# A hybrid attention trunk on one core: five of the query projections by seven products, and what is done around them

## The chip, the cores and the metric

One Trainium2 chip; the kernel uses one of its cores. The metric is the device time of one execution in microseconds, as a median over several runs. TensorE (PE in the profile) does the matrix products, with its weight loads counted apart as PEld; VectorE is DVE, ScalarE is ACT, GpSimd is POOL, SyncE is SP. Each engine works through its own list of instructions in order, and waits on semaphores for the others.

## The reference, cut to what matters

The input of 512 positions is prepended with 16 learned ones and goes through two layers. The first is gated linear attention, which the change does not touch. The second is differential attention in 8 heads, and this is what is computed there (`lam` and `scale` are numbers, `bias` depends on head and distance):

```python
proj = xn @ w_in                     # (528, 1024) @ (1024, 8192)
q, k, v, z = split(proj, 4)          # per head: two q and two k of 128 columns, v and z of 256
s = q_m @ k_m.T * scale + bias       # m = 0, 1; causal
p_m = softmax(s)
a = p_0 - lam * p_1
o = a @ v                            # per head, blocks of 128 queries
o = head_rms(o) * gnorm * (1 - lambda_init)
y = silu(z) * o
h = h + y @ w_out                    # then a final RMS norm, meta positions dropped
```

The 16 prepended positions need keys and values but no queries and no output, so q and z are made for 512 positions and k and v for 528.

## The kernel before, in words

**Numbers.** Every float32 operand of a product is split into a high and a low part (`split`, L276 to L280: ScalarE copies the rounded high part, VectorE subtracts it to get the low one), and a product is the sum high x high + high x low + low x high. `mm3` (L400) does this for small products.

**Two ways to project.** A projection takes 1024 inputs to 256 outputs for one head. `project` (L421) does it plainly: for each half of 128 outputs, 8 blocks of inputs by 3 passes, so 24 matmuls of 512 columns and 48 for a head. Class `Unit` does it as a two by two block product with seven half-sized products in place of eight (Winograd's form): `product` (L431) is one of the seven, 12 matmuls with half of the columns (256 for z, 264 for k and v). Three of the seven results are read out of PSUM by ScalarE (`partial`, L452) and joined to the others by VectorE (`add`, L477 and L479). The weights of a unit need, beside the split of two sums, four sums (`sums` and `outer`, L366) and the splits of three single blocks, `a11`, `a12` and `a22`; plain weights need two splits of 128x1024 only. The corresponding sums of the inputs are made once for all heads (`token_sums2`), and `Xr` is their part without the 16 meta positions. Units chain: a unit that has another behind it in the queue (`nxt`) runs that one's first product (`first`) before its own last ones. One that was begun so (`early`) and has no unit behind it is a lone one: it runs p6, p5, p7, p2, p4, p3. p6 and p7 go to the same PSUM bank `bx`, and p7 may not start before ScalarE has read what p6 left there (u2).

**Head by head.** In the loop over the eight heads the projections of the next head (z, v, k, q in that order; k, q, v, z for the last one) are put into a queue of generators, the `Weaver`. The attention of the present head is a list `steps` of A, B, C and E, each for the four blocks of 128 queries, the longest first. A (`scores`) makes the scores of both m by `mm3`, VectorE adds the bias and takes the minimum (L1692, as the q are negated), ScalarE takes the exponential with the row sums (L1694), VectorE makes the ratio `lam * sum0 / sum1` (L1697, L1698) and subtracts (L1699). B (`turn`) transposes the result on TensorE (L1707, L1708) and splits it. C (`values`) multiplies by v and takes the norm of the row (GpSimd's power -1/2 at L1730, ScalarE's scaling at L1731). E (`rows`) transposes one block (L1737), VectorE multiplies by the gate (L1740), and the result is split into `ys`. Between two steps `W.fill(us)` takes so many estimated microseconds of matmuls out of the queue, so TensorE's list is an order fixed by these shares. The output projection of a pair of heads, `q_diff_out2`, stands first in the queue of heads 2 to 6, so that a head begins with three of its banks and then A of the longest block.

**The other engines' lists.** TensorE's order is the program's. On VectorE, ScalarE, GpSimd and SyncE a scheduler places the instructions, with the priorities that `urgent`, `soon` and `at_once` give (at_once first, soon last). Weights come through SyncE's queue into two `raw` buffers; `Weights` makes the parts of at most two jobs ahead, as the buffers allow.

## Time and profile before

| what | value |
|---|---|
| median of 3 runs | 971.22 us (970.94 to 971.46) |
| the profiled execution: its time, its span | 970.65 us, 968.9 us |
| mean granted TensorE clock | 0.999 |
| PEld busy | 906.9 us (94%) |
| POOL busy, instructions | 44.9 us (5%), 68 |
| bytes moved by DMA | 104.94 MB, 108 GB/s |

The profiled execution's time is 1.75 us more than its span, and 0.57 us less than the median. The gated linear attention fills the first half, up to about 450 us; the scores of the eight heads begin at 500.1, 552.4, 605.0, 667.9, 730.9, 794.0, 857.0 and 911.8 us, so a head's pass is a stretch of about 63 us in the middle.

How to read it: "busy" of PE runs from a matmul's start to its modelled end, which overlaps the next one, so a PE at 100% need not be at its peak; the distance from one start to the next tells its rate. A group's row gives line, engine, operation, tiles and shapes, count, then busy time and mean duration, then the idle time of the engine just before and what ended it.

### The profile page before, as it was taken

What the parts mean: (1) busy time and instruction counts of PE and PEld (TensorE: products, weight loads), DVE (VectorE), ACT (ScalarE), POOL (GpSimd) and SP (SyncE); (2) the same over time, 40 slices, a digit from 0 to 9 for tenths busy, and PEclk for the clock granted to TensorE, in tenths of its full rate; (3) what the DMA queues carried; (4) which work ended last, traced back from release to release, by engine and by line L of the source; (5) the groups of instructions that cost most, each with busy time, mean ns of one, the idle gap of its engine ahead of it and who ended that gap; (6) DMA issues with size and microseconds to landing.
All of it is one profiled execution on the core that took longest, in us unless ns stands there. A gap on an engine that the chain in (4) does not pass through costs nothing.

```text
span 968.9 us, 18048 instructions
## 1 busy us (share of the span) xinstructions
PE 957.2 (99%) x6993; PEld 906.9 (94%) x6993; DVE 778.6 (80%) x1586; ACT 626.8 (65%) x1304; POOL 44.9 (5%) x68
## 2 busy tenths in 40 slices
PE   9999999999999999999999999999999999999997
PEld 8999999999999999998899998998999989989996
DVE  7989885886888787668997987968869769687785
ACT  7776755577647567656757776575675756755583
POOL 1000000000000000000001001000000000000001
PEclk9999999999999999999999999999999999999999
DMA  7322223635363236124355525243342341722212
GB/s 197 88 85 59 82 79 122 147 103 128 116 162 91 85 117 158 53 101 152 99 130 138 143 73 133 75 139 98 99 138 88 118 119 44 182 70 84 89 64 87
DMA packets 128522, 104.94 MB, mean 108 GB/s; under 512 B 51102, under 2 KB 112830, under 8 KB 128433
## 3 DMA queue, kind: packets, MB, share of 16 engines
q1 hardware_dynamic: 123104, 93.80, 35.1%
q10 hardware_dynamic: 5328, 9.95, 2.8%
q8 instruction: 56, 0.92, 0.4%
q14 instruction: 34, 0.27, 0.1%
HBM read 83.64 MB, written 11.80 MB: 99 GB/s over the span
## 4 chain that ended last, share of the span: by engine, by line
PE 88%; ACT 1%; DVE 1%; issue 1%; POOLq 0%; DVEq 0%
PE bx L431 19%; PE bv L431 12%; PE by L431 10%; PE bx L421 10%; PE ps L400 9%; PE bx L972 5%; PE bx L400 3%; PE bv L972 2%; PE by L972 2%; PE ps L1214 2%; PE by L400 2%; PE bv L400 2%; PE ps L1807 1%; PE bx L1807 1%; PE bv L421 1%; PE by L421 1%
## 5 line engine op out<-in xcount | busy, mean ns | idle before, releaser
L277 DVE TENSOR_TENSOR wl<-raw,wh 128x1024 fp32r<-128x1024 f32 x98 | 119.4, 1221 | 23.0 <-ACT wh L276 18.9
L276 ACT ACTIVATE wh<-raw 128x1024 fp32r<-128x1024 f32 x98 | 103.1, 1054 | 48.3 <-PE by L972 22.9
L431 PE MATMUL bv<-x,wh 128*128 128x264 f32 (+1 forms) x656 | 98.6, 287 | 0.0
L431 PE MATMUL bx<-x,wh 128*128 128x264 f32 (+1 forms) x640 | 95.6, 286 | 0.0
L431 PEld LDWEIGHTS bv<-x,wh 128*128 128x128 f32 x656 | 86.8, 189 | 0.6 <-DVE z L479 0.2
L431 PEld LDWEIGHTS bx<-x,wh 128*128 128x128 f32 x640 | 84.6, 188 | 0.7 <-ACT u L452 0.2
L452 ACT ACTIVATE u<-bx 128x264 f32<-128x264 f32 (+1 forms) x120 | 45.3, 379 | 35.5 <-PE bx L431 33.1
L1694 ACT ACTIVATE p<-p,st 128x528 f32<-128x528 f32 (+3 forms) x64 | 36.5, 570 | 41.7 <-DVE st L1692 41.4
L421 PE MATMUL bx<-x,wh 128*128 128x512 f32 (+1 forms) x256 | 62.4, 385 | 0.0
L277 DVE TENSOR_TENSOR wl<-sum,wh 128x1024 fp32r<-128x1024 f32 x41 | 50.1, 1221 | 10.6 <-ACT wh L276 10.5
L431 PE MATMUL bx<-x,wl 128*128 128x264 f32 (+1 forms) x320 | 54.1, 284 | 0.0
L431 PE MATMUL bv<-x,wl 128*128 128x264 f32 (+1 forms) x328 | 53.8, 284 | 0.1
L421 PEld LDWEIGHTS bx<-x,wh 128*128 128x128 f32 x256 | 44.4, 188 | 7.8
L276 ACT ACTIVATE wh<-sum 128x1024 fp32r<-128x1024 f32 x41 | 43.1, 1051 | 9.7 <-PE by L972 3.9
L431 PE MATMUL by<-x,a12h 128*128 128x264 f32 (+1 forms) x320 | 47.5, 286 | 0.1
L1730 POOL TENSOR_TENSOR st<-st,mhalf 128x1 f32<-128x1 f32 x32 | 25.5, 795 | 468.6 <-ACT on L1728 418.2
L431 PE MATMUL bx<-x,a11h 128*128 128x264 f32 (+1 forms) x320 | 46.6, 284 | 0.0
L431 PEld LDWEIGHTS bv<-x,wl 128*128 128x128 f32 x328 | 45.4, 188 | 0.3 <-issue 0.3
L431 PEld LDWEIGHTS bx<-x,wl 128*128 128x128 f32 x320 | 45.3, 188 | 0.3
L431 PEld LDWEIGHTS bx<-x,a11h 128*128 128x128 f32 x320 | 42.4, 188 | 0.6
L431 PEld LDWEIGHTS by<-x,a12h 128*128 128x128 f32 x320 | 42.1, 188 | 0.3 <-ACT t L1658 0.3
L276 ACT ACTIVATE a11h<-raw 128x512 fp32r<-128x512 f32 x41 | 25.7, 626 | 20.7 <-DMA raw<-in_diff_w_in_dram 7.9
(493 smaller groups left out, 2631.9 us busy)
## 6 DMA issues: line engine op xcount, KB each, us to landing
raw<-in_gla_w_in_dram SPq DMA_DIRECT2D x48, 512.0 KB, 4.5
raw<-in_diff_w_in_dram SPq DMA_DIRECT2D x42, 512.0 KB, 4.9
raw<-in_diff_w_in_dram SPq DMA_DIRECT2D x11, 1024.0 KB, 5.9
raw<-in_gla_w_out_dram SPq DMA_DIRECT2D x8, 1024.0 KB, 5.8
raw<-in_diff_w_out_dram SPq DMA_DIRECT2D x8, 1024.0 KB, 6.0
vd<-planes ACTq DMA_DIRECT2D x12, 268.0 KB, 5.8
vd<-keep ACTq DMA_DIRECT2D x12, 264.0 KB, 2.3
T<-bdr SPq DMA_DIRECT2D x8, 264.0 KB, 4.7
```

The source lines that it names most:

```text
L276: act.activation(hi, src, AF.Copy)
L277: dve.tensor_tensor(lo, src, hi.bitcast(F32), op=ALU.subtract)
L400: pe.matmul(ps, l, r, start=first and n == 0, stop=last and n == 2, **kw)
L421: pe.matmul(bank, a[:, k, :], b[k] if n0 is None else b[k][:, n0 + i * nn:n0 + (i + 1) * nn], start=n == 0 and ks[0] == 0, stop=n == len(t ...
L431: pe.matmul(bank[:, :x[q].shape[2]], w[p][:, k * P:(k + 1) * P], x[q][:, k, :], start=first and i == 0, stop=i == len(PASSES) - 1, skip_gr ...
L452: W.moved = act.activation(t, self.bx[:, :self.n], AF.Copy, scale=self.sc)
L972: pe.matmul(banks[i][:, :HT], h.t[p][:, k, mm * P:(mm + 1) * P], s.y[q][k][:, i * HT:(i + 1) * HT], start=n == 0, stop=n == len(PASSES) - 1)
L1214: pe.matmul(o, s.kd[:, i, kc], s.qs[:, i, t0:t0 + n], start=i == 0, stop=i == 1)
L1694: act.activation(p[:, :nk], p[:, :nk], AF.Exp, scale=-1.0, bias=st[:, m:m + 1], accum_out=st[:, 2 + m:3 + m])
L1730: pool.tensor_tensor(ms, ms, mhalf[:, :1], op=ALU.pow)
L1807: pe.matmul(ps[i], yp[hd][p][:, k, b * P:(b + 1) * P], wt[q][cs.start // 512][:, 2 * hd + k, cs.start % 512:(cs.stop - 1) % 512 + 1], star ...
```

## The change

Four things are edited.

1. `q_diff_q`: for heads 3 to 7 the query projection is a `Unit` on `Xr`, as z is, and no longer plain. Its result goes to two scratch tiles `t`, which are split into q with the lower priority of `soon`. Heads 0 to 2 stay plain. TensorE's list loses 240 matmuls of 512 columns and gets 420 of 256; all its other matmuls keep their number and shape, and k of these heads now has a unit behind it, so that q is the lone unit where k was (for head 7, v follows q, and z is the lone one as before). SyncE loads the same bytes of these weights as two transfers of 512 KB in place of one of 1 MB.
2. `scores`: m = 1 is done before m = 0, and the ratio is made by three GpSimd instructions on 128x1 (power -1 of the sum of m = 1, then two products) in place of VectorE's reciprocal and product. `minus` is a new constant.
3. `rows` takes two blocks together (heads 0 to 6): four transposes into one PSUM tile, one product with the gate on 128x512, one split. `steps` has 14 entries in place of 16.
4. The order: in a lone unit a step that is due within 1.6 us of the end of p5 is put just there, between p5 and p7 (`Gap`, `to_gap`, and `fill`). The fill at the start of a head is 4.0 in place of 3.0.

```diff
@@ Weaver.fill
             us -= c
             self.left -= c
             self.spent(c)
+            if isinstance(c, Gap) and us < 1.6:
+                return
+            if us <= 0 and 0 < getattr(self.queue[0], "to_gap", 0) < 1.6:
+                us = 0.01
...
@@ Unit.run
             def p5():
                 self.bv = pb_tile("bv")
-                yield from product(self.bv, ws.use(s21)[1], X["t1"])
+                alone = early and nxt is None
+                self.to_gap = 1.4 if alone else 0
+                for c in product(self.bv, ws.use(s21)[1], X["t1"]):
+                    self.to_gap -= c
+                    if alone and self.to_gap < 0.2:
+                        self.to_gap = 0
+                        c = Gap(c)
+                    yield c
...
     def q_diff_q(hd, s):
+        scale, qts = -float(P) ** -0.5, []
+
+        def tiles():
+            assert not hd or heads[hd - 1].scored
+            s.q = [T(ep, [P, 2, NR], F32R, f"q{j}", bufs=1) for j in range(2)]
+
+        if hd in (3, 4, 5, 6, 7):
+            def dst():
+                tiles()
+                qts.extend([tok_tile()[:, :NR], tok_tile()[:, :NR]])
+                return qts
+
+            @soon
+            def tail(i):
+                split(*[t[:, i, :] for t in s.q], qts[i])
+
+            return W.add(Unit(want_unit(d_w_in, 256 * hd), Xr, scale, dst, tail), 8.9)
         want_diff(256 * hd)
...
@@ scores
-            for m in range(2):
+            for m in (1, 0):
...
-            dve.reciprocal(st[:, 5:6], st[:, 3:4])
-            dve.scalar_tensor_tensor(st[:, 5:6], st[:, 5:6], lam, st[:, 2:3], op0=ALU.mult, op1=ALU.mult)
+                r.p[m] = p[:, :nk]
+
+            pool.tensor_tensor(st[:, 5:6], st[:, 3:4], minus, op=ALU.pow)
+            pool.tensor_tensor(st[:, 4:5], st[:, 2:3], lam, op=ALU.mult)
+            pool.tensor_tensor(st[:, 5:6], st[:, 5:6], st[:, 4:5], op=ALU.mult)
             dve.scalar_tensor_tensor(r.p[0], r.p[1], st[:, 5:6], r.p[0], op0=ALU.mult, op1=ALU.subtract)
...
-        def rows(r):
+        def rows(*rs):
+            w = P * len(rs)
             pt = ps_tile()
             for m in range(2):
-                pe.transpose(pt[:, m * P:(m + 1) * P], r.on[:, m * P:(m + 1) * P], ident)
-            y = T(ep, [P, 2, P], F32, "yt")
-            cs = slice(r.ta, r.ta + P)
-            W.mark = dve.tensor_tensor(y, pt[:, :256].rearrange("p (m c) -> p m c", m=2), s.z[:, :, cs], op=ALU.mult)
+                for j, r in enumerate(rs):
+                    pe.transpose(pt[:, m * w + j * P:m * w + (j + 1) * P], r.on[:, m * P:(m + 1) * P], ident)
+            y = T(ep, [P, 2, w], F32, "yt", bufs=1)
+            cs = slice(rs[0].ta, rs[0].ta + w)
+            W.mark = dve.tensor_tensor(y, pt[:, :2 * w].rearrange("p (m c) -> p m c", m=2), s.z[:, :, cs], op=ALU.mult)
             split(ys[hd][0][:, :, cs], ys[hd][1][:, :, cs], y)
...
-        return A, lambda b: turn(R[b]), lambda b: values(R[b]), lambda b: rows(R[b])
+        return A, lambda b: turn(R[b]), lambda b: values(R[b]), lambda b: rows(*([R[b]] if hd == D_HEADS - 1 else [R[b], R[b + 1]]))
...
-        steps = [(A, 0), (A, 1), (B, 0), (A, 2), (C, 0), (B, 1), (E, 0), (A, 3), (C, 1), (B, 2), (E, 1), (C, 2), (B, 3),
-                 (E, 2), (C, 3), (E, 3)]
+        steps = [(A, 0), (A, 1), (B, 0), (A, 2), (C, 0), (B, 1), (A, 3), (C, 1), (B, 2), (E, 1), (C, 2), (B, 3),
+                 (C, 3), (E, 3)]
...
-        W.fill(3.0)
+        W.fill(4.0)
```

Two places show how the lists move. The first is VectorE at the longest block of the scores of the fifth head's pass (`heads[4]`), before: `ISA p<-ps,T` is the sum with the bias and the minimum (its second row, on `st`, reads the minimum out), `st` holds the sums, `p` the scores.

```order
L1692 ISA p_12028,st_12015<-ps_12029,T_11624 128x264
L1692 ISA st_12015 128x1
L1692 ISA p_12028,st_12015<-ps_12034,T_11624,st_12015 128x264
L1692 ISA st_12015 128x1
L1697 RECIPROCAL st_12015<-st_12015 128x1
L1698 SCALAR_TENSOR_TENSOR st_12015<-st_12015,lam 128x1
L1699 SCALAR_TENSOR_TENSOR p_12016<-p_12028,st_12015,p_12016 128x528
L277 TENSOR_TENSOR wl_12052<-sum_11986,wh_12051 128x1024
```

The same place on VectorE in the changed kernel; L1734 there is L1699 of before, L592, L421 and L286 are splits of v, of its meta rows and of weights.

```order
L1726 ISA p_12142,st_12129<-ps_12148,T_11658,st_12129 128x264
L1726 ISA st_12129 128x1
L592 TENSOR_TENSOR v_2167_12119<-planes_11751,v_2166_12118 128x4x128
L421 SCALAR_TENSOR_TENSOR vm_12120<-lands_12080,short,vm_12120 32x256
L286 TENSOR_TENSOR a22l_12230<-raw_12082,a22h_12229 128x512
L1734 SCALAR_TENSOR_TENSOR p_12142<-p_12130,st_12129,p_12142 128x528
L286 TENSOR_TENSOR wl_12167<-sum_12100,wh_12166 128x1024
```

The two small instructions on `st` are gone, and three others stand between the last reading of the minimum and the subtraction; the subtraction now needs GpSimd's last product, and the split of the weights `wl` stands behind it.

The second place is TensorE in the lone unit of the same pass, before: `wh_11632,wl_11633` against x_1542 is p6, against x_1541 p5; bank `bx_11655` with x_1543 is p7, and L1737 are the transposes of E.

```order
L431 MATMUL bx_11655<-x_1542_8785,wh_11632 128x264 x5
L431 MATMUL bx_11655<-x_1542_8785,wl_11633 128x264 x4
L431 MATMUL bv_11757<-x_1541_8784,wh_11632 128x264 x8
L431 MATMUL bv_11757<-x_1541_8784,wl_11633 128x264 x4
L431 MATMUL bx_11655<-x_1543_8786,wh_11718 128x264 x3
L1737 MATMUL ps_11777<-ident,on_11685 128x128 x2
```

TensorE in the lone unit of the same pass in the changed kernel, which is q: again p6 and p5, then E of two blocks (L1774).

```order
L440 MATMUL bx_11891<-x_1542_8787,wh_11868 128x256 x8
L440 MATMUL bx_11891<-x_1542_8787,wl_11869 128x256 x4
L440 MATMUL bv_11986<-x_1541_8786,wh_11868 128x256 x8
L440 MATMUL bv_11986<-x_1541_8786,wl_11869 128x256 x4
L1774 MATMUL ps_11999<-ident,on_11944 128x128
L1774 MATMUL ps_11999<-ident,on_11854 128x128
```

Before, p7 followed p5 at once and the transposes came three matmuls into p7; now the four transposes stand whole between p5 and p7.

More of the change, by code (lines that the diff above doesn't have):

```diff
@@ L144, in settle @@
                 self.late.pop(0)[1]()
+class Gap(float):
+    pass
 class Part:
@@ L625, in trunk @@
     dve.memset(mhalf, -0.5)
+    minus = cp.tile([P, 1], F32, name="minus")
+    dve.memset(minus, -1.0)
     warm = ps_tile()
```

8 lines of the change are left out of this document (3 added, 5 removed).

## The prediction

> **What bounds the kernel now.** I read the page first, for the engines' shares.
>
> ```profile
> span 968.9 us, 18048 instructions
> PE 957.2 (99%) x6993; PEld 906.9 (94%) x6993; DVE 778.6 (80%) x1586; ACT 626.8 (65%) x1304; POOL 44.9 (5%) x68
> ```
>
> Then the busy time by stretch, cut at the first scores of four heads, since the change lies there.
>
> ```profile
> core 0: us, PE busy (x) PEld busy (x) DVE busy (x) ACT busy (x) POOL busy (x), PEclk, DMA share, GB/s
> 667.87:730.90 63.03, 63.03 (x436) 58.70 (x434) 49.96 (x109) 41.14 (x92) 2.97 (x4) 1.00 0.35 107
> 730.90:793.99 63.09, 63.09 (x435) 58.70 (x434) 48.76 (x108) 40.86 (x92) 3.15 (x4) 1.00 0.37 107
> 793.99:857.03 63.04, 63.04 (x435) 58.74 (x434) 48.92 (x107) 39.20 (x90) 2.61 (x4) 1.00 0.41 113
> ```
>
> TensorE has no idle time in a pass of 63.0 us, at full clock; VectorE rests for 13 to 14 us of it, ScalarE for 22 to 24. So a matmul taken from TensorE's list is time gained, as long as the others keep up. Since a busy PE can hide short waits, I took the rates from starts, in the chain of waits (first row: a plain q; the next two: a lone unit's p7 and the product behind it) and in TensorE's timeline (the rest).
>
> ```profile
> 787.14 2.79 PE bx L421 x12
> 529.24 1.63 PE bx L431 x12
> 530.88 1.47 PE by L431 x12
> ...
> 682.80 1.10 PE L431 MATMUL bv<-x,wh 128*128 128x256 f32 x8
> 683.74 0.64 PE L431 MATMUL bv<-x,wl 128*128 128x256 f32 x4
> 684.22 1.10 PE L431 MATMUL bx<-x,wh 128*128 128x256 f32 x8
> ```
>
> A matmul of 512 columns takes 2.79/12 = 0.2325 us. A product of 12 matmuls of 256 takes 684.22 - 682.80 = 1.42 us, 0.118 each.
>
> **TensorE's part.** For a changed head 48 x 0.2325 = 11.16 us go and 7 x 1.42 = 9.94 us come: 1.22 us less, 6.1 us for five. All other matmuls stay. This lies on the path, so the gain before losses is 6.1 us.
>
> The Trainium skill, "TensorE: Matmul & The Clock Gate", section "Back-to-back issue gap", speaks against this: it gives about 81 ns for a matmul of 128 columns and about 131 ns for one of 512 in a stream of weight loads and matmuls. By a straight line between these, an estimate, 256 columns would take 98 ns, and the sum would be 48 x 0.131 = 6.3 us gone and 84 x 0.098 = 8.2 us come. The rows above disagree for the long ones (232 ns), so the sum goes by the rows.
>
> **VectorE's part.** The groups by shape between 500 and 950 us, and one row of its waits there:
>
> ```profile
> L277 DVE TENSOR_TENSOR a11l<-raw,a11h 128x512 fp32r<-128x512 f32 x19 | 13.1, 689 | 9.3 <-ACT a11h L276 9.1
> L366 DVE TENSOR_TENSOR sum<-raw 128x512 f32<-128x512 f32 x19 | 13.0, 684 | 2.6 <-DMA raw<-in_diff_w_in_dram 2.6
> L280 DVE SCALAR_TENSOR_TENSOR q<-bx,q 128x512 fp32r<-128x512 f32 x14 | 9.6, 684 | 0.3 <-ACT q L279 0.3
> L277 DVE TENSOR_TENSOR hT<-yt,hT 128x256 fp32r<-128x256 f32 x22 | 9.2, 420 | 2.7 <-ACT hT L276 2.6
> L1698 DVE SCALAR_TENSOR_TENSOR st<-st,lam 128x1 f32<-128x1 f32 x32 | 6.9, 216 | 0.6
> L1697 DVE RECIPROCAL st<-st 128x1 f32<-128x1 f32 x32 | 5.1, 158 | 9.4 <-ACT p L1694 9.4
> L479 DVE TENSOR_TENSOR t<-by,u 128x256 f32<-128x256 f32 x7 | 2.9, 415 | 0.0
> ...
> DVE st L1697 <- ACT p L1694: 9.4, 11, 1.8
> ```
>
> A changed head adds three splits of single blocks (3 x 0.689), four sums of weights (4 x 0.684), four joinings (4 x 0.415) and two splits of q from scratch (as a block's, 2 x 0.689), and loses two of q from PSUM (2 x 0.684): +6.47 us. The weights' two big splits stay. Every head loses 4 x (0.216 + 0.158) = 1.50 us of ratios. Rows by twos: eight instructions of about 0.420 become four of 128x512, about 0.684: -0.62 us. So a pass with a changed q has 49.96 + 6.47 - 1.50 - 0.62 = 54.3 us of VectorE in 61.8 us, 88%.
>
> On top come waits. The subtraction of the scores (L1699) now needs ScalarE's exponential and then two GpSimd products in a row, and whatever VectorE has behind it stands too: weight splits, joinings that free PSUM banks for TensorE. From the timeline of the last short block, VectorE's reading of the minimum, the exponential, then GpSimd between two ScalarE instructions:
>
> ```profile
> 939.59 0.08 DVE L1692 DVE_READ_ACCUMULATOR2_ANT st<- 128x1 f32 x1
> 939.70 0.42 ACT L1694 ACTIVATE p<-p,st 128x144 f32<-128x144 f32 x1 [0.32 <-DVE st L1692]
> 940.02 0.18 ACT L1694 ACTIVATION_READ_ACCUMULATOR p<-p,st 128x1 f32 x1
> 940.63 0.19 ACT L1728 ACTIVATION_READ_ACCUMULATOR on<-ps 128x1 f32 x1
> 940.96 0.55 POOL L1730 TENSOR_TENSOR st<-st,mhalf 128x1 f32<-128x1 f32 x1 [7.17 <-issue]
> 941.54 0.47 ACT L1731 ACTIVATE on<-ps,st 128x256 f32<-128x256 f32 x1 [0.72 <-POOL st L1730]
> ...
> 570.63 2.27 POOL L1730 TENSOR_TENSOR st<-st,mhalf 128x1 f32<-128x1 f32 x1 [24.76 <-ACT on L1728]
> 570.67 1.22 DVE L277 TENSOR_TENSOR wl<-sum,wh 128x1024 fp32r<-128x1024 f32 x1
> ```
>
> From the minimum (939.67) to the sum (940.20) 0.53 us; to GpSimd 0.14; its instruction 0.55; back to another engine 0.03. A product on GpSimd isn't in the trace; the bounds are nothing and the 2.27 us above, and I take the 0.55 of a power. The power of m = 1 lies beside the exponential of m = 0. So the subtraction can start 0.53 + 0.14 + 2 x 0.55 + 0.03 = 1.8 us after the minimum of a short block, some 0.3 later for a long one. The new order puts none to three other instructions between, about 1.2 us on average by the durations above, so a wait of w = 0.6 to 0.9 us is left; I take w = 1.0, four in a pass. In place of it go the 9.4 us of L1697's waits in eight passes, 1.2 a pass. TensorE needs the result in B, at least one step and two fills later (over 5 us by its estimates), so it loses nothing directly.
>
> What does such a full VectorE cost TensorE? The fullest stretch of before is in the first layer, where units follow each other:
>
> ```profile
> 60.00:70.00 10.00, 10.00 (x84) 10.00 (x84) 10.00 (x18) 7.62 (x16) 0.00 (x0) 1.00 0.06 7
> 70.00:80.00 10.00, 9.85 (x81) 9.46 (x80) 9.79 (x18) 5.50 (x9) 0.00 (x0) 1.00 0.29 101
> 80.00:90.00 10.00, 9.85 (x83) 9.66 (x82) 9.60 (x18) 4.40 (x9) 0.00 (x0) 1.00 0.39 111
> ```
>
> VectorE at 29.4 of 30 us, TensorE idle 0.3: 1%. Over five new units of 10 us that is 0.5 us, my term for new losses. Its cover is the weights made ahead; without it a unit would wait for them.
>
> **ScalarE's part.**
>
> ```profile
> L276 ACT ACTIVATE a11h<-raw 128x512 fp32r<-128x512 f32 x19 | 11.8, 624 | 8.3 <-DMA raw<-in_diff_w_in_dram 7.9 <-PE bx L431 0.4
> L279 ACT ACTIVATE q<-bx 128x512 fp32r<-128x512 f32 x14 | 8.2, 586 | 0.4 <-PE bx L421 0.3
> L452 ACT ACTIVATE u<-bx 128x256 f32<-128x256 f32 x20 | 7.5, 377 | 13.0 <-PE bx L431 13.0
> ```
>
> Five copies (3 blocks, 2 of q) and three readings, less two of q: 5 x 0.624 + 3 x 0.377 - 2 x 0.586 = +3.1 us on 41 of 62: hidden by its 20 us of rest.
>
> **The rest.** The gap: the lone unit's p7 of the chain above took 1.63 us where its neighbour took 1.47, so at most 0.16 us a pass can go, 0.8 for five; four transposes there also cover for u2. I count nothing and keep 0.8 for the range. The fill of 4.0 takes as many pieces of the output projection (1.4 each, three pass 3.0 and 4.0) in heads 2 to 6, and moves order only elsewhere: nothing. Two transfers of 512 KB land no later than one of 1 MB; the queue before them is as long. At the end, A of the shortest block holds VectorE some 0.8 us longer (1.8 after the minimum where L1699 now starts 1.0 after it), beside TensorE's products: at most that, inside the range.
>
> **Sum.** 970.65 - 6.1 + 0.5 = 965.05 us for the profiled execution; from the median of 971.22 us, 5.6 less is 965.6 us.
>
> **Rivals.** *The seam of the heads.* The new q goes through joining, ScalarE and VectorE, with lower priority, before the next head's scores; TensorE has only three output banks in between. Before, in the timeline of all engines:
>
> ```profile
> 726.68 0.40 PE L400 MATMUL bx<-wh,y 128*128 128x512 f32 x1
> 728.17 0.58 ACT L279 ACTIVATE q<-bx 128x512 fp32r<-128x512 f32 x1
> 729.13 0.68 DVE L280 SCALAR_TENSOR_TENSOR q<-bx,q 128x512 fp32r<-128x512 f32 x1
> ```
>
> q's products end at 726.68, ScalarE comes 1.49 us later, q is ready at 729.81, 3.13 us after, and the scores start at 730.90: 1.09 us to spare. Joining adds about 0.2 + 0.415 and waits. For it: the queues that made these 1.49 us grow. Against: m = 1 now goes first, and its half of q comes a product (1.42 us) earlier, while m = 0 has its six scores of 264 columns more. If 0.8 us are lost at each of five seams, 4.0 of 5.6 us go: 969.6 us.
>
> *VectorE becomes the bound, slower.* A pass of VectorE is 54.3 + 4w + r, r being what it rests anyway; in the full stretch above 2%, 1.2 us. It passes 63.04 where w is over (63.04 - 54.3 - 1.2)/4 = 1.9 us. For it: GpSimd took 2.27 us beside VectorE's split. Against: VectorE stands still as it waits, which leaves GpSimd its 0.55. With no instruction between and a GpSimd product at 0.86, w = 2.5: 65.5 us a pass, 2.5 us more in each of five, 983.7 us.
>
> The Trainium skill, "SBUF — State Buffer", section "Who interferes with whom", has a VectorE instruction with two SBUF inputs and a GpSimd one that reads SBUF exclude each other, the first to start blocking the other. In the rows above GpSimd started first, and VectorE's split kept its 1.22 us: the trace bears out only half of it. By the whole rule three more GpSimd instructions a step would hold VectorE 4 x 3 x 0.55 = 6.6 us a pass, an estimate with the trace's duration, and bring this rival's point near without any w.
>
> *The short matmuls are dear.* More matmuls mean more weight loads, from the page's groups:
>
> ```profile
> L431 PEld LDWEIGHTS bv<-x,wh 128*128 128x128 f32 x656 | 86.8, 189 | 0.6 <-DVE z L479 0.2
> ```
>
> If 256 columns cost more than 11.16/84 = 0.133 us in q, the exchange loses. If a weight load sets the pace there, 84 x 0.189 = 15.9 us, 4.7 more a head, 23.6 in all: 994.8 us. The 0.118 of the same form in z, and the 0.136 of the slow p7, speak against it.
>
> By the Trainium skill's rule of the gap, above, the loss would be 1.9 us a head, and the time an estimated 981 us; the 232 ns of the long matmuls leave it little.
>
> *It doesn't do what it says*, TensorE's list unchanged: 971.2 us; the lists by themselves exclude it.
>
> **How the numbers follow.** About 0.2%, 1.9 us, can be told from no change. Forecast (better included) 0.76, the seam 0.12, VectorE 0.09, short matmuls 0.03. Of the seam's cases half are faster by over 0.2% (under 969.3 us) and half within: faster 0.82, same 0.06, slower 0.12. The low end is 971.22 - 6.1 - 0.8 and 0.3 for the spread of runs, 964.0; the high end is the seam's 969.7. Left out are VectorE, the short matmuls and some of either edge, under 2 in 10.
>
> **What would show it.** Right: a pass of about 61.9 us between first scores; L421 gone from heads 3 to 7; 256-column products at 1.42 us; VectorE at 54 us a pass; L1734 waiting for GpSimd about 1 us. Wrong: TensorE idle ahead of the first scores on q (the seam), or ahead of weights or banks on VectorE (the second), or L1734's waits near 2 us with passes over 63.

## The result, and the profile after

The changed kernel takes 974.16 us (median of 9 runs, 972.19 to 976.48), the kernel before on the same chip 970.94 us (970.35 to 971.46): a ratio of 1.0036, 95% interval 1.0025 to 1.0046. It is slower by a third of a per cent, where 965.6 us was forecast. The profiled execution took 974.99 us.

The shares of the engines, from the page of the changed kernel:

```profile
span 972.1 us, 18486 instructions
PE 953.7 (98%) x7173; PEld 911.9 (94%) x7173; DVE 795.6 (82%) x1550; ACT 637.1 (66%) x1320; POOL 82.9 (9%) x164
```

TensorE's busy time fell by 3.5 us, but its idle time (span less busy) rose from 968.9 - 957.2 = 11.7 us to 972.1 - 953.7 = 18.4. Busy time also hides short waits. The whole loss is the span's +3.2 us and the 6.1 us that TensorE's own work should have lost: 9.3 us. The stretches, cut at the first scores of the eight heads, show where it lies:

```profile
502.18:556.79 54.61, 53.01 (x388) 49.80 (x387) 42.95 (x90) 37.53 (x88) 8.13 (x16) 1.00 0.66 148
556.79:608.19 51.40, 51.40 (x367) 48.37 (x366) 40.72 (x87) 36.79 (x86) 8.84 (x16) 1.00 0.35 102
608.19:670.21 62.02, 62.02 (x471) 59.84 (x471) 51.62 (x103) 40.72 (x92) 8.52 (x16) 1.00 0.37 109
670.21:733.41 63.20, 62.40 (x471) 59.91 (x471) 55.53 (x112) 43.19 (x97) 7.61 (x16) 1.00 0.36 108
733.41:795.61 62.20, 62.12 (x471) 59.81 (x471) 53.57 (x106) 42.35 (x96) 7.86 (x16) 1.00 0.37 109
795.61:859.61 64.00, 62.45 (x472) 59.90 (x471) 52.71 (x107) 42.45 (x95) 7.79 (x16) 1.00 0.38 108
859.61:916.51 56.90, 56.28 (x387) 51.76 (x386) 49.24 (x97) 34.98 (x83) 7.18 (x16) 1.00 0.25 79
```

With 1.22 us less, the four passes of 62.9 to 63.1 us before should take 61.7 to 61.9. The third pass takes 62.02, 0.9 us less than its 62.90 before, so most of what the exchange is worth shows there; the next three lose about 1.4, 0.3 and 2.2 us again. The other losses lie at the ends. The first two passes take 106.0 us where 104.8 stood, although three pieces of a unit (9 matmuls of 264 columns, some 1.1 us) now come before the first scores: 2.3 us lost. The last two take 112.5 us where 111.87 - 1.2 was due: 1.8 us. The remaining 0.9 us lies before the first scores; profiled executions of kernels whose TensorE lists are the same up to there begin them between 499.7 and 500.7 us, so this is no sure loss.

What TensorE waited for between 500 and 960 us, in the view of waits (total, times, longest), before:

```profile
PE ps L400 <- DVE yt L1740: 0.2, 1, 0.2
```

and after:

```profile
PE bx L440 <- ACT u L461: 1.4, 2, 0.8
PE ps L409 <- DVE aT L286: 1.0, 1, 1.0
PE ps L409 <- ACT aT L285: 0.9, 2, 0.6
PE bv L440 <- DVE t L488: 0.7, 1, 0.7
PE ps L409 <- DVE am L419: 0.4, 1, 0.4
PE by L440 <- DVE t L486: 0.2, 1, 0.2
PE bx L409 <- DVE keep L1820: 0.2, 1, 0.2
```

They are several kinds of small waits, each for a reading, a split or a joining on ScalarE or VectorE, 4.8 us in all; the rest of the 9.3 us shows in no wait of this view. The largest kind, in the fourth pass, in the timeline of all engines (u is the reading of p6 that frees the bank for p7; the unit here is the first of the pass, that of z, which the change leaves as it was):

```profile
684.13 0.91 PE L409 MATMUL ps<-k,q 128*128 128x272 f32 x6
684.88 0.52 PE L440 MATMUL bx<-x,wl 128*128 128x256 f32 x3
685.30 0.68 DVE L375 TENSOR_TENSOR sum<-raw 128x512 f32<-128x512 f32 x1
685.90 0.43 DVE L1726 CUSTOM_DVE_ANT_0 p<-ps,T 128x272 f32<-128x272 f32 x1
686.18 0.64 PE L440 MATMUL bv<-x,wl 128*128 128x256 f32 x4
686.43 0.52 ACT L1728 ACTIVATE p<-p,st 128x272 f32<-128x272 f32 x1 [3.00 <-DVE st L1726]
686.96 0.36 ACT L461 ACTIVATE u<-bx 128x256 f32<-128x256 f32 x1
687.37 1.21 PE L440 MATMUL bx<-x,wh 128*128 128x256 f32 x8 [0.55 <-ACT u L461]
```

The scores end at 685.0, but VectorE has a sum and splits of a later unit's weights ahead of their minimum. ScalarE stands 3.00 us at the exponential. Behind it in ScalarE's list is u, whose product p6 (the row at 684.88) ended at 685.40, and TensorE waits for u.

### The profile page after: what moved, and what is told of

Same layout as the page of the kernel before. It is cut to its first block, busy times and chain, and to the rows that moved or that the text cites. A ratio compares the mean times of both kernels' runs of the same rounds, so it can differ in the third digit from the quotient of the medians.

```text
span 972.1 us, 18486 instructions
## 1 busy us (share of the span) xinstructions
PE 953.7 (98%) x7173; PEld 911.9 (94%) x7173; DVE 795.6 (82%) x1550; ACT 637.1 (66%) x1320; POOL 82.9 (9%) x164
## 4 chain that ended last, share of the span: by engine, by line
PE 68%; DVE 10%; ACT 5%; DMA 4%; issue 2%; POOL 1%; SPq 0%; POOLq 0%; DVEq 0%; ACTq 0%
PE bx L440 17%; PE by L440 10%; PE bv L440 10%; PE ps L409 7%; PE bx L430 4%; PE bx L990 4%; DMA raw<-in_diff_w_in_dram 3%; DVE wl L286 2%; PE by L990 2%; PE bv L990 2%; PE bx L409 2%; PE ps L1232 2%; DVE sum L375 1%; ACT wh L285 1%; DMA raw<-in_gla_w_in_dram 1%
## 5 line engine op out<-in xcount | busy, mean ns | idle before, releaser
L286 DVE TENSOR_TENSOR wl<-raw,wh 128x1024 fp32r<-128x1024 f32 x93 | 113.4, 1220 | 14.5 <-ACT wh L285 13.8
L440 PE MATMUL bv<-x,wh 128*128 128x264 f32 (+1 forms) x736 | 108.7, 286 | 0.8 <-DVE t L488 0.7
L440 PE MATMUL bx<-x,wh 128*128 128x264 f32 (+1 forms) x720 | 105.8, 286 | 1.4 <-ACT u L461 1.4
L440 PEld LDWEIGHTS bv<-x,wh 128*128 128x128 f32 x736 | 96.6, 188 | 1.8 <-DVE t L488 0.9
L440 PEld LDWEIGHTS bx<-x,wh 128*128 128x128 f32 x720 | 94.3, 188 | 2.8 <-ACT u L461 2.3
L286 DVE TENSOR_TENSOR wl<-sum,wh 128x1024 fp32r<-128x1024 f32 x46 | 56.2, 1221 | 13.0 <-ACT wh L285 12.2
L440 PE MATMUL bv<-x,wl 128*128 128x264 f32 (+1 forms) x368 | 61.4, 285 | 0.1
L440 PE MATMUL by<-x,a12h 128*128 128x264 f32 (+1 forms) x360 | 53.9, 286 | 0.5 <-DVE t L486 0.2
L440 PE MATMUL bx<-x,a11h 128*128 128x264 f32 (+1 forms) x360 | 53.5, 285 | 0.0
L1731 POOL TENSOR_TENSOR st<-st,minus 128x1 f32<-128x1 f32 x32 | 21.6, 676 | 289.9 <-ACT p L1728 289.9
L558 POOL TENSOR_TENSOR st<-st,mhalf 128x1 f32<-128x1 f32 (+1 forms) x20 | 12.1, 606 | 387.5 <-DVE st L557 387.5
L375 DVE TENSOR_TENSOR sum<-raw 128x512 f32<-128x512 f32 x46 | 31.6, 687 | 13.6 <-DMA raw<-in_diff_w_in_dram 7.7
```

Source lines behind the costliest of these rows:

```text
L286: dve.tensor_tensor(lo, src, hi.bitcast(F32), op=ALU.subtract)
L375: dve.tensor_tensor(o, a, b, op=ALU.add)
L440: pe.matmul(bank[:, :x[q].shape[2]], w[p][:, k * P:(k + 1) * P], x[q][:, k, :], start=first and i == 0, stop=i == len(PASSES) - 1, skip_gr ...
L558: pool.tensor_tensor(dst, dst, mhalf[:np_, :dst.shape[1]], op=ALU.pow)
L1731: pool.tensor_tensor(st[:, 5:6], st[:, 3:4], minus, op=ALU.pow)
```

## The experiments

All times are medians; every kernel was timed beside the kernel before (970.46 to 970.55 us), and the ratio is to that. The first four take the change apart.

**Edit 1 alone**: q by units in heads 3 to 7, put into the kernel before.

```diff
+        if hd in (3, 4, 5, 6, 7):
...
+            return W.add(Unit(want_unit(d_w_in, 256 * hd), Xr, scale, dst, tail), 8.9)
```

> The kernel before with the first edit alone: q of heads 3 to 7 by seven products; ratio, rows, steps and fills as before. Theory 1 (the wait for GpSimd: VectorE stands at L1734 and is late for all that is behind it): without GpSimd's ratio the gain of TensorE comes out, 965 to 967 us. Theory 2 (the units' own work: four sums, three splits and four joinings a head fill VectorE, so that ScalarE stands at the exponentials and TensorE behind it): the loss is here too, 970 to 974 us. Theory 3 (the order: rows by two, 14 steps, the gap and the fill put steps where their inputs are not ready): 965 to 967 us, as under theory 1.

970.07 us, ratio 0.9996 (0.9987 to 1.0005). So of the 6.1 us nothing is left that can be measured, without the other edits. By the starts of the scores, its third and sixth pass do take 61.84 and 61.89 us, about 1.1 less than before; the fourth, fifth and seventh take 63.37, 63.15 and 56.05, more than before (63.03, 63.09 and 54.80). TensorE's waits between 500 and 960 us are 3.1 us in all in place of 0.2, the longest 0.8 for u and 0.8 for `yt`.

**Edit 2 alone**: m = 1 first and the ratio on GpSimd.

```diff
-            dve.reciprocal(st[:, 5:6], st[:, 3:4])
-            dve.scalar_tensor_tensor(st[:, 5:6], st[:, 5:6], lam, st[:, 2:3], op0=ALU.mult, op1=ALU.mult)
+            pool.tensor_tensor(st[:, 5:6], st[:, 3:4], minus, op=ALU.pow)
+            pool.tensor_tensor(st[:, 4:5], st[:, 2:3], lam, op=ALU.mult)
+            pool.tensor_tensor(st[:, 5:6], st[:, 5:6], st[:, 4:5], op=ALU.mult)
```

> The kernel before with the second edit alone: m = 1 before m = 0, and the ratio on GpSimd. Theory 1: 973 to 976 us, with VectorE waiting some 17 us for GpSimd in the eight passes, as in the changed kernel. Theory 2: 970.5 to 972 us, since VectorE has rest enough in every pass to take these waits. Theory 3: 970.5 to 972 us.

974.53 us, 1.0040 (1.0026 to 1.0054). An edit that takes 1.5 us a pass from VectorE, and nothing from or to TensorE, costs 4.1 us.

Where it goes can be seen, since TensorE's list is that of before, instruction by instruction. ScalarE's list differs in four places only: in z's unit of the passes 3 to 6, u has moved from ahead of the two exponentials of the third block to between them (VectorE's list differs in many more). The sixth pass, in the timeline before:

```profile
809.22 0.38 ACT L452 ACTIVATE u<-bx 128x256 f32<-128x256 f32 x1 [1.45 <-PE bx L431]
809.97 0.65 PE L431 MATMUL bv<-x,wl 128*128 128x256 f32 x4
810.45 1.10 PE L431 MATMUL bx<-x,wh 128*128 128x256 f32 x8
```

and with edit 2:

```profile
812.51 0.64 PE L431 MATMUL bv<-x,wl 128*128 128x256 f32 x4
813.61 0.52 ACT L1696 ACTIVATE p<-p,st 128x272 f32<-128x272 f32 x1 [3.29 <-DVE st L1694]
814.13 0.36 ACT L452 ACTIVATE u<-bx 128x256 f32<-128x256 f32 x1
814.55 1.21 PE L431 MATMUL bx<-x,wh 128*128 128x256 f32 x8 [1.40 <-ACT u L452]
```

From p5's last four matmuls to p7 it is 0.48 us before (809.97 to 810.45) and 2.04 us here. In the passes 3 to 5 it is 0.48 us each before, and 0.67, 0.68 and 1.80 us here, so these four places make 3.3 of the 4.1 us.

**Edit 3 alone**: rows of two blocks together.

```diff
+        def rows(*rs):
...
+        steps = [(A, 0), (A, 1), (B, 0), (A, 2), (C, 0), (B, 1), (A, 3), (C, 1), (B, 2), (E, 1), (C, 2), (B, 3),
+                 (C, 3), (E, 3)]
```

> The kernel before with the third edit alone: output rows of two blocks turned and split together, and 14 steps. Theories 1 and 2: 970 to 971.5 us, a little less work for VectorE and the same for TensorE. Theory 3: 972 to 975 us.

974.97 us, 1.0048 (1.0035 to 1.0062). One of its waits, in the first pass, in the timeline:

```profile
539.15 3.23 POOL L1730 TENSOR_TENSOR st<-st,mhalf 128x1 f32<-128x1 f32 x1 [8.88 <-ACT on L1728]
539.54 1.22 DVE L277 TENSOR_TENSOR wl<-raw,wh 128x1024 fp32r<-128x1024 f32 x1
...
542.41 0.47 ACT L1731 ACTIVATE on<-ps,st 128x256 f32<-128x256 f32 x1 [3.34 <-POOL st L1730]
542.78 0.27 ACT L276 ACTIVATE aT<-ps 128x128 fp32r<-128x128 f32 x1
543.10 0.71 PE L400 MATMUL ps<-v,aT 128*128 128x256 f32 x3 [1.19 <-ACT aT L276]
```

GpSimd's power, 0.55 us in the prediction's row, takes 3.23 us while VectorE runs splits and sums; ScalarE stands at `on`, the copy of the shortest block's `aT` stands behind it, and TensorE waits 1.19 us for that. Another wait, of 1.67 us in the second pass, is for `on` behind a power of 1.56 us. The first three passes, with 53.93, 54.45 and 63.70 us in place of 52.22, 52.61 and 62.90, hold nearly the whole cost. In the best version below, which leaves the rows single in this head, the same power took 0.57 us, and TensorE didn't wait.

**The change with the ratio back on VectorE**, m = 1 still first:

```diff
-            pool.tensor_tensor(st[:, 5:6], st[:, 3:4], minus, op=ALU.pow)
...
+            dve.reciprocal(st[:, 5:6], st[:, 3:4])
+            dve.scalar_tensor_tensor(st[:, 5:6], st[:, 5:6], lam, st[:, 2:3], op0=ALU.mult, op1=ALU.mult)
```

> The changed kernel with the ratio back on VectorE (reciprocal and product), m = 1 still first; the constant for GpSimd is gone with it. Theory 1: 965 to 967 us. Theory 2: 972 to 976 us, no better than the changed kernel, as VectorE gets 12 us of small instructions back. Theory 3: 973 to 975 us.

970.95 us, 1.0003 (0.9994 to 1.0012), outside all three expectations: in company too the ratio costs 974.16 - 970.95 = 3.2 us.

The next four ask what the other parts do in company.

**Without the ratio and the rows by two**: units, gap, fill and m = 1 first. To the edit above comes:

```diff
-        def rows(*rs):
+        def rows(r):
```

> The changed kernel without the second and third edit: units for q, the gap and the fill of 4.0, m = 1 first, ratio on VectorE, rows of single blocks in 16 steps. The theory now (heads of lists: each of the three edits makes VectorE or ScalarE stand at an instruction whose input is late, and TensorE stands for what is queued behind it; the stalls add up where they fall at different places): without rows by two the stalls of the first two passes go, 966 to 968 us. The rival (VectorE is simply full in passes 2 to 6, whatever the order): as the units alone, 969 to 971 us.

972.34 us, 1.0017 (1.0009 to 1.0026). Both expectations missed: by the medians it is slower than with the rows by two (970.95; the intervals overlap a little), though those alone cost 4.5 us.

**Ratio on VectorE, rows by two only in heads 2 to 6**:

```diff
-rows(*([R[b]] if hd == D_HEADS - 1 else [R[b], R[b + 1]]))
+rows(*([R[b], R[b + 1]] if 2 <= hd < D_HEADS - 1 else [R[b]]))
```

> The changed kernel with the ratio on VectorE, and rows by two in heads 2 to 6 only (single blocks and 16 steps in the others). Theory of the heads of lists: rows by two cost in the first two passes and the last, where a plain q still stands, and save VectorE 0.6 us a pass in the others: 966 to 968 us, no worse than with single rows everywhere. Rival (VectorE full): 969 to 971 us.

969.62 us, 0.9990 (0.9981 to 0.9999), in the rival's range and not the theory's. It differs from the kernel with single rows everywhere (972.34) by the rows of heads 2 to 6 alone, and the intervals lie apart: beside q's units the rows by two help, by 2.7 us. That they hurt in the first two heads, where q is plain, is so by the medians only (970.95 and 969.62, overlapping a little).

**The change without the gap and with a fill of 3.0:**

```diff
-            if isinstance(c, Gap) and us < 1.6:
-                return
...
-        W.fill(4.0)
+        W.fill(3.0)
```

> The changed kernel without its fourth edit: no step put into the lone unit's gap, fill of 3.0. Theory of the heads of lists: rows by two then stand at the old places and cost as they do alone: 975 to 979 us. Rival (VectorE full): 973 to 975 us, as the changed kernel.

976.81 us, 1.0066 (1.0054 to 1.0078): gap and fill together give 2.7 us, where I had counted nothing. The two weren't parted.

**The change with plain q:**

```diff
-        if hd in (3, 4, 5, 6, 7):
...
-            return W.add(Unit(want_unit(d_w_in, 256 * hd), Xr, scale, dst, tail), 8.9)
```

> The changed kernel without its first edit: all q plain, with ratio on GpSimd, rows by two, the gap and the fill. Theory of the heads of lists: TensorE gets its 6 us back, and the stalls of ratio and rows stay: 975 to 979 us. Rival (VectorE full): with 6.5 us less for VectorE a changed pass the stalls vanish, 970.5 to 973 us.

975.55 us, 1.0053 (1.0040 to 1.0066). By the medians the units are worth 975.55 - 974.16 = 1.4 us in company, of the 5.6 forecast (the intervals overlap a little). This kernel has the ratio on GpSimd too, and VectorE waits 23.8 us for it between 500 and 955 us; yet its passes 4 to 6 take 63.06, 63.13 and 63.02 us, no more than before. In all four places of z's unit, u stands ahead of the exponentials here. What it loses lies in the first two passes and the seventh.

So each of the first three edits costs stalls, and they don't add. The next runs test what makes them.

**More work on VectorE, nothing else**: the kernel before, with a part of q's plain weights split again.

```diff
+        wh, wl = split_w(raw, ca)
+        for i in range(n):
+            ks = slice(4 * (i % 2), 4 * (i % 2) + 4)
+            dve.tensor_tensor(wl[:, ks, :], raw[:, ks, ca:ca + P], wh[:, ks, :].bitcast(F32), op=ALU.subtract)
```

> The kernel before, and nothing of the change: only VectorE is given more to do. Where the plain weights of q for heads 3 to 7 are made, the low part is subtracted again in nine pieces of 128x512 (about 0.689 us each by the group of L277, 6.2 us a head), which changes no value. TensorE's list stays as it was. Theory (a fuller VectorE comes late, ScalarE's list then stands at the exponential, and TensorE behind both): VectorE at 56 us of a pass, as with the units, and TensorE stalls without any unit for q, +2 to +4.5 us, 973 to 975. Rival (what the units lose comes from their own links: p7 behind u, joinings before banks come free): plain q lets the scores wait for nothing more, 970.5 to 971.5.

971.92 us, 1.0018 (1.0009 to 1.0027), between the two. The stretch of three middle passes, as in the windows of the prediction, decides:

```profile
668.00:857.00 189.00, 189.00 (x1303) 176.03 (x1302) 165.25 (x354) 121.12 (x274) 11.30 (x12) 1.00 0.37 107
```

VectorE is busy for 165.25 of 189 us, more than in the changed kernel (162.21), and TensorE doesn't lose anything there: it makes 1303 matmuls in the stretch, as before. What the profiled execution (973.81 us) loses comes in the last pass, with waits of 1.1 us for `aT` and 0.9 for the meta rows; there ScalarE stands at `on` again, behind a power of 1.60 us. **So in these three passes a fuller VectorE alone doesn't stall TensorE**; my theory had that wrong.

**Less work on VectorE, but a longer chain**: edit 1 alone, with the four sums of q's weights on GpSimd.

```diff
-            dve.tensor_tensor(o, a, b, op=ALU.add)
+            (eng or dve).tensor_tensor(o, a, b, op=ALU.add)
```

> The kernel before with the q of heads 3 to 7 by units and nothing else of the change (970.07 us so far), and the four sums of 128x512 of q's weights made by GpSimd in place of VectorE (4 x 0.684 = 2.7 us a head off VectorE). TensorE's list is the same. Theory (VectorE is late because it is full): the stalls above the count's own error, 1.5 and 1.3 us in passes 3 and 4 and 1 us in pass 6, halve or more, 967 to 968.7. Rival 1 (the units' own links are what stalls): 969.6 to 970.5. Rival 2 (GpSimd's sums are slow and hold VectorE's or the weights up): over 971.

978.26 us, 1.0078 (1.0064 to 1.0091), the second rival. The same stretch:

```profile
668.00:857.00 189.00, 184.12 (x1376) 175.46 (x1377) 158.47 (x343) 126.19 (x290) 25.77 (x24) 1.00 0.36 103
```

Edit 1 alone, with the sums on VectorE, has VectorE busy for 166.05 us of this stretch and TensorE idle for 1.3. Here VectorE does 7.6 us less, and TensorE stands idle for 4.9. What counts is when a result comes, not how full the engine is.

**A shorter chain for the ratio**, the product with `lam` beside the exponential:

```diff
-            pool.tensor_tensor(st[:, 4:5], st[:, 2:3], lam, op=ALU.mult)
-            pool.tensor_tensor(st[:, 5:6], st[:, 5:6], st[:, 4:5], op=ALU.mult)
+            pool.tensor_tensor(st[:, 5:6], st[:, 5:6], lam, op=ALU.mult)
+            pool.tensor_tensor(st[:, 5:6], st[:, 5:6], st[:, 2:3], op=ALU.mult)
```

> The changed kernel; TensorE's list is the same. Of the ratio's three GpSimd instructions the product with lam is moved: it now multiplies the power of the first sum, beside the exponential of the other m, so that only the last product (about 0.2 us) stands between the second sum and VectorE, and not two (0.66 + 0.2). Theory (VectorE's wait of 0.7 us for GpSimd, four times a pass, is what the ratio costs, by what stands behind it): the wait falls to 0.1 to 0.3 us and 1.5 to 3 us of the 3.2 that parted the changed kernel from the one with the ratio on VectorE come back, 971 to 972.7. Rival (the ratio's cost lies in the order of the lists that came out otherwise, or in GpSimd's work beside VectorE's): 973.5 to 975.

973.61 us, 1.0036 (1.0024 to 1.0048): no difference from the change that can be measured. VectorE's waits for the last product, between 500 and 955 us, in the change and then here:

```profile
DVE p L1734 <- POOL st L1733: 17.4, 25, 2.1
```

```profile
DVE p L1734 <- POOL st L1733: 17.7, 26, 2.2
```

They didn't shorten, and the product that was moved had been short already (0.3 us on the mean). That what they follow, the exponential's sum, is what comes late is my reading and wasn't tried.

**A fill of 3.0 in heads 0, 1 and 7** on top of rows by two only in the middle and the ratio on VectorE:

```diff
-        W.fill(4.0)
+        W.fill(4.0 if 2 <= hd < D_HEADS - 1 else 3.0)
```

> The kernel with q by units, the gap, the ratio on VectorE and rows by two only in heads 2 to 6 (969.62 us), with the fill at a head's start of 3.0 in heads 0, 1 and 7 as before. If the fill of 4.0 only moves a unit's work ahead in the first two heads, where nothing is short, no difference, 969.2 to 970. If it keeps E or aT from ending late there (stall of 1.4 us in the first pass against 2.1 to 3.5 where it was 3.0 with rows by two), it loses up to 1 us, 970 to 970.8.

968.82 us, 0.9985 (0.9976 to 0.9994): below both expectations, and the best version, faster than both kernels. Against 969.62 us the intervals overlap, so the fill's share isn't shown. All of TensorE's waits there between 500 and 960 us:

```profile
PE ps L409 <- DVE yt L1774: 0.9, 1, 0.9
PE bv L440 <- DVE t L488: 0.7, 1, 0.7
PE ps L409 <- ACT aT L285: 0.3, 1, 0.3
```

**The same with the short ratio on GpSimd:**

```diff
-            dve.reciprocal(st[:, 5:6], st[:, 3:4])
-            dve.scalar_tensor_tensor(st[:, 5:6], st[:, 5:6], lam, st[:, 2:3], op0=ALU.mult, op1=ALU.mult)
+            pool.tensor_tensor(st[:, 5:6], st[:, 3:4], minus, op=ALU.pow)
+            pool.tensor_tensor(st[:, 5:6], st[:, 5:6], lam, op=ALU.mult)
+            pool.tensor_tensor(st[:, 5:6], st[:, 5:6], st[:, 2:3], op=ALU.mult)
```

> As the one above, with the ratio on GpSimd in the short chain (power and the product with lam beside the exponential, one product behind it). Theory (only the wait behind the second sum costs, and VectorE is rid of 1.5 us a pass): no more than with the ratio on VectorE, 968 to 970. Rival (any ratio on GpSimd costs 3 us): 971.5 to 973.

971.31 us, 1.0011 (1.0002 to 1.0020), between the two expectations: 2.5 us for the ratio once more.

Then I saw a difference in the lists. Where the ratio is on VectorE, ScalarE's list has u *ahead* of the exponentials at the place shown above, here in the timeline of the change with the ratio back on VectorE:

```profile
686.59 0.39 ACT L461 ACTIVATE u<-bx 128x256 f32<-128x256 f32 x1 [2.01 <-PE bx L440]
686.98 0.53 ACT L1726 ACTIVATE p<-p,st 128x272 f32<-128x272 f32 x1
687.81 1.11 PE L440 MATMUL bx<-x,wh 128*128 128x256 f32 x8
```

TensorE doesn't wait there, though VectorE's minimum isn't much earlier: it starts 1.16 us after the scores, against 1.77 in the change (684.13 to 685.90, above). The next runs test that order by itself. In the change, the exponentials of the third block are held until u is issued:

```diff
+            held = b == 1 and hd in (3, 4, 5)
...
+                if held:
+                    with tc.issue_after(W.moved.ins):
+                        exps(1)
+                        exps(0)
...
+                W.defer(0.9, lambda: r.rest and urgent(r.rest)())
```

> The changed kernel with u ahead of both exponentials of the third block in heads 3, 4 and 5, as it stands before the change; in the changed kernel it stands between them. Only six instructions of ScalarE's list move; TensorE's, VectorE's and GpSimd's lists are the same. Theory (u behind an exponential that waits for a late VectorE is what stops p7): the waits of 0.55 and 0.81 us for u go, and passes 3 to 5 with stalls of 2.0, 1.1 and 2.9 us come to about 0.7, 0.7 and 1.6, 971 to 972.3 us in place of 974.16. Rival (VectorE's lateness is the cause, and what waits is only the first to show it): the stall moves to the next instruction, 973.5 to 974.5.

973.39 us (971.05 to 978.62), 1.0038 (1.0022 to 1.0053), between the two expectations. At the place shown, in the timeline:

```profile
684.46 0.39 ACT L461 ACTIVATE u<-bx 128x256 f32<-128x256 f32 x1 [2.00 <-PE bx L440]
685.20 0.64 PE L440 MATMUL bv<-x,wl 128*128 128x256 f32 x4
685.67 1.11 PE L440 MATMUL bx<-x,wh 128*128 128x256 f32 x8
```

TensorE's waits for u are gone, all 1.4 us, and passes 4 to 6 take 62.4, 61.9 and 63.5 us in place of 63.2, 62.2 and 64.0. The profiled execution took 971.05 us. But the medians, 974.16 and 973.39, have intervals that overlap, so a gain isn't shown by time.

The exponentials with a higher priority, so that u stands behind both:

```diff
-                act.activation(p[:, :nk], p[:, :nk], AF.Exp,
+                urgent(act.activation, 130)(p[:, :nk], p[:, :nk], AF.Exp,
```

> The changed kernel with the exponentials at a higher priority, so that u stands behind both exponentials of the third block in heads 3, 4 and 5 and not between them: an exponential of 0.5 us more ahead of it. TensorE's and GpSimd's lists are the same. Theory: u 0.4 to 0.5 us later in each of three passes, 0.8 to 1.5 us more in all, 974.9 to 975.7. Rival (u's place does not matter): 973.8 to 974.5.

972.78 us, 1.0022 (1.0012 to 1.0032): by the medians less than the change, against both expectations. The wait grew as the theory has it:

```profile
PE bx L440 <- ACT u L461: 3.7, 3, 1.9
```

3.7 us in place of 1.4; but the priority held everywhere, and the first pass took 53.1 us in place of 54.6, where `aT`, for one, came earlier.

Put together, in these kernels the time from p5's last four matmuls to p7 (start to start, in the timelines) goes with u's place:

| kernel | u and the two exponentials | passes 3 to 6, us |
|---|---|---|
| before | ahead | 0.48, 0.48, 0.48, 0.48 |
| edit 2 alone | between | 0.67, 0.68, 1.80, 2.04 |
| the change | ahead in pass 3, then between | 0.48, 1.19, 0.72, 1.45 |
| the change with plain q | ahead | 0.48, 0.48, 0.48, 0.48 |
| the change, u held ahead | ahead | 0.48, 0.47, 0.48, 0.48 |
| the change, u behind both | ahead in pass 3, then behind | 0.48, 1.28, 2.52, 1.87 |

In the change this makes 1.9 us; held ahead, u gives them back at these places. Standing behind an exponential costs time only where that exponential is late: edit 1 alone and the change with the ratio on VectorE have places with u between the two or behind them, and 0.48 us or less there.

The order of u in edit 1 alone, held in the four passes that have q's unit and such a block:

```diff
+            held = b == 1 and hd in (2, 3, 4, 5)
```

> The kernel before with the q of heads 3 to 7 by units and nothing else of the change (970.07 us so far), and u ahead of both exponentials of the third block in heads 2 to 5. TensorE's list is the same. Theory: the stalls of passes 3 and 4 (2.2 and 2.0) fall to 0.7, 966.5 to 968.3. Rival (the units lose by joinings and by VectorE, wherever u stands): 969.4 to 970.5.

970.22 us, 0.9998 (0.9989 to 1.0006), the rival. Its largest wait for u is at another place, that of p1's result, in the timeline:

```profile
677.64 0.63 ACT L1705 ACTIVATE p<-p,st 128x400 f32<-128x400 f32 x1 [1.11 <-DVE st L1713]
...
680.78 0.36 ACT L452 ACTIVATE u<-bx 128x256 f32<-128x256 f32 x1
681.20 0.97 PE L431 MATMUL bx<-x,wh 128*128 128x256 f32 x6 [0.77 <-ACT u L452]
```

u is again behind what came after a late exponential: a weight copy of 1.05 us, `aT`, the meta rows, `a11h`.

The order of u with the short ratio and rows by two in the middle heads:

```diff
+            held = b == 1 and hd in (3, 4, 5)
```

> The kernel with q by units, the gap, rows by two only in heads 2 to 6, the fill of 3.0 in heads 0, 1 and 7, and the ratio on GpSimd in the short chain (971.31 us so far), with u put ahead of the exponentials in heads 3, 4 and 5. Theory (the ratio on GpSimd cost what it cost because u came to stand behind the exponential in two more passes): it falls to that of the same kernel with the ratio on VectorE, 968 to 969.7. Rival (GpSimd's wait itself costs): 970.5 to 971.5.

970.73 us, 1.0002 (0.9994 to 1.0011): 0.6 us less than without, intervals overlapping; 1.9 us remain between it and the same kernel with the ratio on VectorE. So here u's place is one of the links, and not the whole cost of the ratio; in the fourth pass, which gained only 0.1 us (62.74 to 62.63), a wait of 0.25 us for a joining stands in its place.

Last, the best version with u put ahead in its one pass where it still stood between:

```diff
+            held = b == 1 and hd == 5
```

> The kernel with q by units, the gap, the ratio on VectorE, rows by two in heads 2 to 6 and the fill of 3.0 in heads 0, 1 and 7 (968.82 us), with u put ahead of the exponentials in the one pass where it still stands between them, that of head 5. No single wait of over 0.5 us for u shows in that pass, so what is to be had is small: 968.2 to 968.8 if u's place costs anything there, 968.8 to 969.2 if not.

968.88 us, 0.9984 (0.9975 to 0.9993): no difference. That pass had only 0.2 us to lose between p5 and p7 (0.67 where 0.48 stands elsewhere).

## Why the prediction was wrong

**TensorE's part: right.** Where no stall falls, a pass with q by a unit is shorter by nearly the 1.22 us: the third and sixth of edit 1 alone by 1.06 and 1.15 (61.84 and 61.89 us), the fourth and fifth of the best version by 1.16 and 1.20 (61.87 and 61.89). The 256-column products keep their rate: in the timeline of the changed kernel, from p2's first matmul to the next product's is 683.07 - 681.64 = 1.43 us, against 1.42.

```profile
681.64 1.12 PE L440 MATMUL by<-x,a12h 128*128 128x256 f32 x8
683.07 1.10 PE L440 MATMUL bx<-x,wh 128*128 128x256 f32 x8
```

The rival of the dear short matmuls falls with it.

**VectorE's work: right.** 54.3 us a pass were forecast, from a base of 49.96; the passes 3 to 6 show 51.6 to 55.5, 53.4 on the mean.

**The wait w: smaller than forecast.** 17.4 us over 32 steps are 0.54 a step, where 1.0 was taken. The rival of VectorE as the bound, which decides at 1.9, falls.

**The step that failed: "VectorE at 29.4 of 30 us, TensorE idle 0.3: 1%. Over five new units of 10 us that is 0.5 us, my term for new losses."** It was 5.7 us for edit 1 alone (6.1 forecast on TensorE, 0.4 gained by the medians), and 9.3 us for the whole change. The step took a loss to be a matter of how full VectorE is. The extra splits show that it isn't (165 of 189 us, no loss in that stretch), and the sums on GpSimd show the reverse (158 of 189 us, 4.9 us lost). The runs showed this in its place: in the attention passes, the lists hold work for TensorE behind work that waits for another engine, and there a late result costs TensorE time however full the engine is. The clearest link is u behind an exponential: 1.9 us in the change, 3.3 in edit 2 alone. The term had no row from a pass with scores in it. Edits 2 and 3 had no term for TensorE at all in the sum; alone they cost 4.1 and 4.5 us.

**"TensorE needs the result in B ... so it loses nothing directly"** and ScalarE **"hidden by its 20 us of rest"** looked at the delayed result alone. What costs time in the places shown is what stands behind it: VectorE late with a minimum, ScalarE standing at the exponential or at `on`, and u, `aT` or `on` behind it. ScalarE's rest is no cover, as it rests *at* such an instruction (3.00 us above), with ready work behind.

**The gap and the fill, "I count nothing":** they give 2.7 us. **The rows by two** had "-0.62 us" of VectorE's work a pass and nothing else; they cost 4.5 us alone, and left to the middle heads they gave 2.7 us beside the units (972.34 to 969.62). For TensorE's time such edits count by the order that they make.

**The seam of the heads** shows no wait for q in the changed kernel's view of waits, and one of 0.2 us in edit 1 alone.

What is shown: the wait for u goes and comes with its place on ScalarE's list, with TensorE's list unchanged. For the ratio alone this is the greater part of the cost by the traces, though no run put u ahead in that kernel; and with plain q and u ahead, the ratio on GpSimd cost nothing in the passes 4 to 6. What stays open is the ratio's cost beside q's units: neither the length of GpSimd's chain (973.61 against 974.16) nor u's place (973.39, and 970.73 against 968.82) accounts for more than a part by the medians, and m = 1 first with a ratio on VectorE doesn't carry it (970.95). The remaining stalls of the units, and those of the rows by two beyond the two shown, were not traced to an order by an experiment.

## What to carry to other kernels

When TensorE is the bound and the other engines have rest, price an edit by what stands behind each late instruction on its in-order list, not by the busy share: look in the timeline for the rests of the helper engines, see which instruction they rest at, and which ready work behind it TensorE needs next. Time each edit alone and in company, since here three edits of +4.5, +4.1 and -0.4 us and an order worth -2.7 made +3.2 together; leaving out the ratio on GpSimd, and the rows by two and the larger fill where q is plain, made -1.7 of it.

## What the runs showed of the hardware

GpSimd's last product on 128x1 costs little, its power more; the groups of the changed kernel between 500 and 960 us:

```profile
L1731 POOL TENSOR_TENSOR st<-st,minus 128x1 f32<-128x1 f32 x32 | 21.6, 676 | 289.9 <-ACT p L1728 289.9
L1733 POOL TENSOR_TENSOR st<-st 128x1 f32<-128x1 f32 x32 | 6.5, 204 | 2.5
```

0.20 us for this product, where the prediction took the power's 0.55.

GpSimd and VectorE hold each other up, in both directions. The power took 3.23 us beside VectorE's splits (edit 3 alone, above). With the sums on GpSimd, a split of VectorE's that takes 0.69 us took 1.25, its end just 0.56 us behind the end of GpSimd's first sum:

```profile
704.54 1.28 POOL L366 TENSOR_TENSOR sum<-raw 128x512 f32<-128x512 f32 x1 [11.91 <-DVE p L1715]
705.13 1.25 DVE L277 TENSOR_TENSOR a11l<-raw,a11h 128x512 fp32r<-128x512 f32 x1 [0.63 <-PE bx L431]
```

The Trainium skill, "SBUF — State Buffer", section "Who interferes with whom", says that a VectorE instruction with two SBUF inputs and a GpSimd one that reads SBUF shut each other out. The rows agree that either can be the one held up. That the first to start blocks the other isn't borne out by the power of 3.23 us, as it wasn't by the prediction's row: its record starts at 539.15 us, VectorE's split starts 0.39 us later and keeps its 1.22. A 128x512 sum takes 1.28 us on GpSimd and 0.68 on VectorE.

The changed kernels spread more than the one before: 972.19 to 976.48 us against 970.35 to 971.46, and with u ahead 971.05 to 978.62. There the longest runs are those with the lowest granted clock (978.62 us at 0.994, 976.10 at 0.996, 971.05 and 971.33 at 0.999); why stays open.
